# Two projection groups fed side by side, half rows of x first, and six warming products instead of eight

## The chip, the cores and the metric

One core of one Trainium2 chip. The metric is the device time of one execution in microseconds (us), the median of three runs. Engines: TensorE (PE in the profile) multiplies, ScalarE (ACT) and VectorE (DVE) work on tiles, GpSimd (POOL) does small work, SyncE (SP) issues most DMAs. PSUM has eight banks of 128 x 512 float32.

## The reference

A decoder block with two attention branches that read the same normalised input. What this case touches is its first step, the input projection:

```python
h = rms_norm(x, norm_g[layer])            # x: 512 x 1024
proj = h @ w_in[layer]                    # 1024 x 6152
fq, fk, fv, fz, mq, mk, mv, mz, ga, gb, fl = split_cols(proj, IN_SPLITS)
q = rms_norm(to_heads(fq, FOX_HEADS), fox_q_g[layer])
k = rms_norm(to_heads(fk, FOX_HEADS), fox_k_g[layer])
log_f = jax.nn.log_sigmoid((fl + b_f[layer]).astype(jnp.float32)).transpose(0, 2, 1)
...
merged = (jax.nn.sigmoid(ga + b_gate[layer, 0]) * (y_fox @ w_fox[layer])
          + jax.nn.sigmoid(gb + b_gate[layer, 1]) * (y_moba @ w_moba[layer]))
x = x + merged @ w_out[layer]
```

`fq` and `fk` are 512 columns each, `fl` is 8. All is float32.

## The kernel before

The hidden dimension of 1024 is cut into 8 slices of 128 rows (`KT`, index k), the sequence of 512 into 4 tiles of 128 (`NT`, index t), the columns of the weights into groups of 256 (`CW`). A group has a name: `fqa` is the first half of the columns of fq, `fka` the first half of fk, `fza`, `fzb` those of fz, `fva` of fv, and so on. `fka` carries the 8 columns of fl (tile `wfl`) too, so its products are 264 columns wide.

To keep float32 accuracy each operand is split into a high and a low part of type float32r, and each product is made of three: high x high, high x low, low x high. The high part of a weight chunk (`wh_...`) is a copy by ACT (or by DVE), the low part (`wl_...`) a subtraction by DVE; for x they are `Zh` (ACT, scaled by the norm weight) and `Zl` (DVE), one pair for each k (`split_x`, L121 to L126). The first three groups of columns use these un-normalised Z; the row statistics (`x_stats`, L218, from which `r` comes) are put in later: `norm_row` (L234, tile `p_rbc`) turns r into a row, and `normalise` (L240) makes `Gh` and `Gl`, which all later groups use.

`first_loads` (L65) issues the first DMAs: the constants `cs` on ACT's queue, all else on SP's, weight chunks of `fqa` (k=0, k=1, k=2 and 3, k=4 to 7) between the slices `xt` of x. Eight DMAs can be on their way: each later one waits until the one eight before it has landed. `first_split` (L148) makes the two parts of the fqa chunks, with `split_x` between them, `load_fl` (L139) loads and splits `fka` in two chunks of 4 slices. `first_qk` (L371) then runs over k, and for each k over the four t, with three products each, into four banks: first all of `fqa`, in the banks of the tags `pj` and `lg`, then all of `fka`, in the banks `tp` and `pv`. `evac_qk` (L307) copies each bank out on ACT; `fza` takes the `pj` banks next, `p_rbc` an `lg` bank, `fzb` a `tp` bank. Before the data are there, PE runs `WARM` = 8 products on a tile of zeros (L106).

The text of the program gives priorities; the order of instructions on each engine is then fixed by a scheduler when the program is built, and each engine takes its own in that order. Two places later in the program matter: `p_LR` (L489), which ends the forget gate's work and opens the attention of the first heads, and attention itself, where products of the next groups (`fqb`, `fkb`, ...) are put between as filling.

Of the kernel before, what the change touches and what calls it, by code (L numbers as in the profile page):

```python
# [7 lines left out]
F32 = mybir.dt.float32  # L8
F32R = mybir.dt.float32r
AF = mybir.ActivationFunctionType  # L10
OP = mybir.AluOpType
AX = mybir.AxisListType

P = 128
S = 512
D = 1024
NT = S // P
KT = D // P
HD = 64
CW = 256  # L20
EPS = 1e-6
NEG = -3.0e38
WARM = 8
WR = 4

C_NG, C_BG, C_FQ, C_FK, C_MQ, C_MK, C_BF, C_GQ, C_GK, C_END = 0, 8, 24, 25, 26, 27, 28, 36, 52, 68
# [3 lines left out]
def fox_moba_kernel(ctx: ExitStack, tc, xT, x, w_in, w_fl, w_fox, w_moba, w_out, cst, rope, out):  # L30


    nc = tc.nc
    V, A, G, T = nc.vector, nc.scalar, nc.gpsimd, nc.tensor

    con = ctx.enter_context(tc.tile_pool(name="con", bufs=1))
    sb = ctx.enter_context(tc.tile_pool(name="sb", bufs=1))
# [3 lines left out]
    stage = {}  # L41
# [7 lines left out]
    def t2(tag, bufs, name, shape=(P, 512), dt=F32):  # L49
        pool = stage["pool"] if tag in ("qs", "pt", "pc", "ys") else sb  # L50
        return pool.tile(list(shape), dt, name=name, tag=tag, bufs=bufs)

    def pst(tag, bufs, name):
        return ps.tile([P, 512], F32, name=name, tag=tag, bufs=bufs)
# [5 lines left out]
        return pst("tp", 3, name)  # L60


    XT, RAW = {}, {}

    def first_loads():  # L65
        def xt(eng, k):
            XT[k] = t2("y", 15, f"xt{k}")
            eng.dma_start(out=XT[k], in_=xT[:, k, :])

        def w(k0, k1):  # L70
            hf = k0 // 4
            if hf not in RAW:
                RAW[hf] = sb.tile([P, 4, CW], F32, name=f"wr_fqa{hf}", tag="wr", bufs=WR)
            nc.sync.dma_start(out=RAW[hf][:, k0 - 4 * hf:k1 - 4 * hf], in_=w_in[0, :, k0:k1, :])
        nc.scalar.dma_start(out=cs, in_=cst)
        w(0, 1)
        xt(nc.sync, 0)
        w(1, 2)
        xt(nc.sync, 1)
        w(2, 4)  # L80
        xt(nc.sync, 2)
        xt(nc.sync, 3)
        w(4, 8)
        for k in range(4, KT):
            xt(nc.sync, k)


    cs = con.tile([P, C_END], F32, name="cs")
# [16 lines left out]
    wps = pst("tp", 3, "warm_ps")  # L105
    for i in range(WARM):  # L106
        T.matmul(wps, warm[:, :P], warm, start=True, stop=True)
# [10 lines left out]
    Gl = con.tile([P, KT, S], F32R, name="Gl")  # L118
    Z = {}

    def split_x(*ks):  # L121
        for k in ks:
            xt = XT[k]
            zh, zl = Z[k] = [stage["pool"].tile([P, S], F32R, name=f"Z{hl}{k}") for hl in "hl"]
            A.activation(zh, xt, AF.Copy, scale=col(C_NG + k))
            V.scalar_tensor_tensor(zl, xt, col(C_NG + k), zh.bitcast(F32), op0=OP.mult, op1=OP.subtract)  # L126


    chunks = {}

    def split(src, n, name, half=False):
        hi = sb.tile([P, 4, 264], F32R, name=f"wh_{name}", tag="wh", bufs=4)
        lo = sb.tile([P, 4, 264], F32R, name=f"wl_{name}", tag="wl", bufs=4)
        A.activation(hi[:, :, 0:n], src, AF.Copy)  # L134
        for eng, q in ((V, slice(0, 2)), (G, slice(2, 4))) if half else ((V, slice(0, 4)),):
            eng.tensor_tensor(out=lo[:, q, 0:n], in0=src[:, q], in1=hi[:, q, 0:n].bitcast(F32), op=OP.subtract)  # L136
        return hi, lo

    def load_fl(name, c0, hf):  # L139
        raw = sb.tile([P, 4, CW], F32, name=f"wr_{name}{hf}", tag="qk", bufs=4)  # L140
        nc.sync.dma_start(out=raw, in_=w_in[c0 // CW, :, 4 * hf:4 * hf + 4, :])
        hi, lo = split(raw, CW, f"{name}{hf}")
        f = wfl[:, 4 * hf:4 * hf + 4, :]
        A.activation(hi[:, :, CW:264], f, AF.Copy)
        V.tensor_tensor(out=lo[:, :, CW:264], in0=f, in1=hi[:, :, CW:264].bitcast(F32), op=OP.subtract)
        chunks.setdefault(name, []).append((hi, lo))

    def first_split(hf, between):  # L148
        raw = RAW[hf]
        hi = sb.tile([P, 4, 264], F32R, name=f"wh_fqa{hf}", tag="wh", bufs=4)  # L150
        lo = sb.tile([P, 4, 264], F32R, name=f"wl_fqa{hf}", tag="wl", bufs=4)
        for q, xs in enumerate(between):
            k = slice(2 * q, 2 * q + 2) if hf else slice(max(q, 2 * q - 2), max(q + 1, 2 * q))
            if hf == 0 and q < 2:
                V.tensor_copy(hi[:, k, :CW], raw[:, k])
            else:
                A.activation(hi[:, k, :CW], raw[:, k], AF.Copy)
            V.tensor_tensor(out=lo[:, k, :CW], in0=raw[:, k], in1=hi[:, k, :CW].bitcast(F32), op=OP.subtract)
            split_x(*xs)
        chunks.setdefault("fqa", []).append((hi, lo))  # L160

    COLS = {}
    off = 0
    for nm in ("fq", "fk", "fv", "fz", "mq", "mk", "mv", "mz"):
        for hfn in ("a", "b"):
            COLS[nm + hfn] = off
            off += CW
    for nm in ("ga", "gb"):
        for i in range(4):
            COLS[f"{nm}{i}"] = off  # L170
            off += CW

# [17 lines left out]
    def stream(name):  # L192
        first_prep[name] = len(preps)
        if name[0] == "G":
            group(name)
            return
        w, n, cnt = ((w_fox, int(name[2]), 1) if name[:2] == "wf" else (w_moba, int(name[2]), 1) if name[:2] == "wm"
                     else (w_out, int(name[2]), 2) if name[:2] == "wo" else (w_in, COLS[name] // CW, 2))
        for hf in range(cnt):
# [18 lines left out]
    def x_stats():  # L218
        G.memset(mh, -0.5)
        for t in range(NT):  # L220
            for hf in range(2):
                xt = t2("y", 15, f"x{t}{hf}")
                nc.sync.dma_start(out=xt, in_=x[t * P:(t + 1) * P, hf * 512:(hf + 1) * 512])
                j = t2("u", 4, "junk")
                A.activation(j, xt, AF.Square, accum_out=ms2[:, t, hf:hf + 1])
        V.tensor_add(mm, ms2[:, :, 0], ms2[:, :, 1])
        V.tensor_scalar(mm, mm, 1.0 / D, EPS, op0=OP.mult, op1=OP.add)
        V.tensor_scalar(e2, mm, EPS, None, op0=OP.mult)
        G.tensor_tensor(out=r, in0=mm, in1=mh[:, :NT], op=OP.pow)
# [138 lines left out]
                        in1=tab[:, ts, None, 24:32].to_broadcast([P, 2, 4, 8]), op=OP.mult)  # L368
        G.tensor_tensor(out=qn[:, :, :, 0:16], in0=ra, in1=rb, op=OP.add)

    def first_qk(name, tags):  # L371
        banks = [pst(tg, n, f"{name}_{i}") for i, (tg, n) in enumerate(tags)]
        n = 264 if name == "fka" else CW
        for kk in range(KT):
            hi, lo = chunks[name][kk // 4]
            k = kk % 4
            for t in range(NT):
                st = slice(t * P, (t + 1) * P)
                T.matmul(banks[t][:, :n], Z[kk][0][:, st], hi[:, k, :n], start=(kk == 0), stop=False)
                T.matmul(banks[t][:, :n], Z[kk][0][:, st], lo[:, k, :n], start=False, stop=False)  # L380
                T.matmul(banks[t][:, :n], Z[kk][1][:, st], hi[:, k, :n], start=False, stop=(kk == KT - 1))
        return banks

    def unit(name, t):
        def go():
# [317 lines left out]
    def group(name):  # L703
# [201 lines left out]
    def seq(names):  # L905
        for u in filler(names):
            u()

    first_split(0, ((0,), (1, 2), (3, 4)))
    first_split(1, ((5, 6), (7,)))  # L910
    nc.sync.dma_start(out=wfl, in_=w_fl)
    load_fl("fka", COLS["fka"], 0)
    load_fl("fka", COLS["fka"], 1)
    b1 = first_qk("fqa", (("pj", 2), ("pj", 2), ("lg", 2), ("lg", 2)))
    b2 = first_qk("fka", (("tp", 3), ("tp", 3), ("tp", 3), ("pv", 1)))
    x_stats()
    for t in range(NT):
        evac_qk(b1[t], "fqa", t)
# [5 lines left out]
    fz = filler(["fza", "fzb"])  # L924
# [119 lines left out]
```

## Time and profile before

| | us |
|---|---|
| median of 3 runs (lowest, highest) | 433.29 (433.22, 433.48) |
| the profiled execution | 432.65 |
| its span | 430.9 |
| PE busy | 424.5 |
| DVE busy | 313.7 |
| ACT busy | 249.6 |
| POOL busy | 86.6 |
| DMA, mean rate over the span | 130 GB/s |

A span is the time from the first to the last record of the profiled execution. The page gives each engine's busy time, and a chain: the work that ended last, followed back from each step to what released it. A timeline row has start, length, engine, line, operation and the tiles written and read; in brackets stands how long the engine was idle before it, and what ended that. A matmul's listed length includes the time until its result is out, so consecutive products overlap in the list.

### The profile page before, as it was taken

The page shows a single profiled execution, that of the slowest core. Times are in us where ns is not written, and L with a number is a line of the kernel's source. Part 1 is how long each engine was busy: PE and PEld are TensorE (multiplying, and loading weights), DVE is VectorE, ACT ScalarE, POOL GpSimd, SP SyncE. Part 2 cuts the span into 40 slices and gives each one's busy share as a digit, 9 for nine tenths or more (in the row PEclk, how much of TensorE's full clock was granted, in tenths as well). Part 3 has the DMA queues.
Part 4 walks back from the last instruction along what each step waited for, and adds up shares of the span by engine and source line. Part 5 has one row for each costly group of instructions (what it writes and reads, how often), then busy time and mean ns, then how long its engine had stood idle before and what let it go on. Part 6 is the DMA issues. An engine that isn't in the chain of part 4 may idle for free.

```text
span 430.9 us, 8095 instructions
## 1 busy us (share of the span) xinstructions
PE 424.5 (99%) x3103; PEld 400.5 (93%) x3103; DVE 313.7 (73%) x559; ACT 249.6 (58%) x480; POOL 86.6 (20%) x108
## 2 busy tenths in 40 slices
PE   8999999999999999999999999999999999999996
PEld 6998899999999998999998878899999989999996
DVE  5679965869979867767856898959897796673311
ACT  4986336876868767677765855547655545531100
POOL 1049200227044660044630003020000000000000
PEclk9999999999999999999999999999999999999999
DMA  7981235326565413303304305561415306525221
GB/s 245 398 293 54 94 102 152 98 79 206 170 213 176 140 39 119 122 13 122 111 15 137 110 13 186 181 196 52 146 50 184 110 3 211 187 96 166 85 92 46
DMA packets 25670, 56.13 MB, mean 130 GB/s; under 512 B 3240, under 2 KB 11872, under 8 KB 25632
## 3 DMA queue, kind: packets, MB, share of 16 engines
q1 hardware_dynamic: 14528, 40.08, 28.0%
q10 hardware_dynamic: 9952, 11.34, 8.8%
q0 software_dynamic: 1152, 4.19, 2.7%
q8 instruction: 24, 0.39, 0.4%
q14 instruction: 14, 0.11, 0.1%
HBM read 46.01 MB, written 6.32 MB: 121 GB/s over the span
## 4 chain that ended last, share of the span: by engine, by line
PE 96%; DVE 2%; DMA 1%; issue 0%; SPq 0%; DVEq 0%
PE pb_GB L750 3%; PE pb_GA L750 3%; PE pb_GB L749 3%; PE pb_GA L747 3%; PE pb_GB L747 3%; PE pb_GA L749 3%; PE po L847 3%; PE po L849 3%; PE po L848 3%; PE pv L608 2%; PE pv L607 2%; PE lg L553 2%; PE lg L552 2%; PE pm L676 2%; PE pm L677 2%; PE pm L678 2%
## 5 line engine op out<-in xcount | busy, mean ns | idle before, releaser
L557 ACT ACTIVATE p<-p,negm 128x128 f32<-128x128 f32 (+1 forms) x64 | 35.7, 558 | 14.4 <-DVE negm L555 12.2
L331 POOL TENSOR_TENSOR ff<-ss,mh 128x8 f32<-128x8 f32 x16 | 27.8, 1743 | 65.5 <-DVE ss L329 65.1
L555 DVE CUSTOM_DVE_ANT_0 p<-lg,mask 128x128 f32<-128x128 f32 (+1 forms) x64 | 30.8, 485 | 13.0 <-PE lg L553 12.3
L847 PE MATMUL po<-wh_wo,mgh 128*128 128x256 f32 x96 | 27.1, 282 | 0.0
L849 PE MATMUL po<-wh_wo,mgl 128*128 128x256 f32 x96 | 27.0, 282 | 0.0
L848 PE MATMUL po<-wl_wo,mgh 128*128 128x256 f32 x96 | 26.9, 281 | 0.0
L857 DVE TENSOR_TENSOR ot<-po,xr 128x256 f32<-128x256 f32 x16 | 6.6, 424 | 24.7 <-PE po L849 23.5
L134 ACT ACTIVATE wh_wo<-wr_wo 128x1024 fp32r<-128x1024 f32 x8 | 8.5, 1061 | 21.6 <-PE po L849 8.0
L552 PE MATMUL lg<-KH,QS 128*128 128x128 f32 (+1 forms) x64 | 20.5, 329 | 0.0
L633 DVE TENSOR_TENSOR ypair<-pv,ysh 64x512 f32<-64x512 f32 x16 | 11.0, 687 | 12.9 <-ACT ysh L632 12.8
L136 DVE TENSOR_TENSOR wl_GB<-wr_gb,wh_GB 128x1024 fp32r<-128x1024 f32 x14 | 16.8, 1224 | 4.2 <-ACT wh_GB L134 3.3
L136 DVE TENSOR_TENSOR wl_GA<-wr_ga,wh_GA 128x1024 fp32r<-128x1024 f32 x14 | 17.9, 1294 | 2.5 <-ACT wh_GA L134 2.4
L134 ACT ACTIVATE wh_GB<-wr_gb 128x1024 fp32r<-128x1024 f32 x14 | 14.6, 1059 | 8.6 <-PE pm L677 2.5
L134 ACT ACTIVATE wh_GA<-wr_ga 128x1024 fp32r<-128x1024 f32 x14 | 14.6, 1059 | 8.5 <-PE pb_GA L749 4.3
L848 PEld LDWEIGHTS po<-wl_wo,mgh 128*128 128x128 f32 x96 | 18.1, 189 | 0.0
L849 PEld LDWEIGHTS po<-wh_wo,mgl 128*128 128x128 f32 x96 | 18.1, 189 | 0.0
L847 PEld LDWEIGHTS po<-wh_wo,mgh 128*128 128x128 f32 x96 | 18.1, 189 | 0.0
L136 DVE TENSOR_TENSOR wl_wo<-wr_wo,wh_wo 128x1024 fp32r<-128x1024 f32 x8 | 9.8, 1222 | 7.4 <-ACT wh_wo L134 7.4
L632 ACT ACTIVATE ysh<-pv 64x512 f32<-64x512 f32 x16 | 9.5, 594 | 8.9 <-PE pv L608 6.4
L604 DVE TENSOR_TENSOR ptl<-p_a,pth 128x512 fp32r<-128x512 f32 x16 | 11.0, 686 | 4.1 <-ACT pth L603 4.1
L676 PE MATMUL pf<-yhf,wh_wf 128*128 128x512 f32 x32 | 13.2, 414 | 0.6 <-DVE zs_mzb L422 0.6
L526 DVE SCALAR_TENSOR_TENSOR QS<-p_qT,cs,QS 64x512 fp32r<-64x512 f32 x16 | 12.0, 750 | 2.5 <-ACT QS L525 2.2
(447 smaller groups left out, 1769.9 us busy)
## 6 DMA issues: line engine op xcount, KB each, us to landing
wr_ga<-in_w_in_dram SPq DMA_DIRECT2D x8, 512.0 KB, 3.5
wr_gb<-in_w_in_dram SPq DMA_DIRECT2D x8, 512.0 KB, 5.0
wr_wo<-in_w_out_dram SPq DMA_DIRECT2D x8, 512.0 KB, 4.2
xt<-in_xT_dram SPq DMA_DIRECT2D x8, 256.0 KB
x<-in_x_dram SPq DMA_DIRECT2D x8, 256.0 KB, 7.2
KH<-KH ACTq DMA_DIRECT2D x16, 128.0 KB, 2.4
s_dramh<-sum_sh ACTq DMA_DIRECT2D x8, 256.0 KB
s_draml<-sum_sl ACTq DMA_DIRECT2D x8, 256.0 KB, 4.4
```

What stands on the lines that cost most here:

```text
L134: A.activation(hi[:, :, 0:n], src, AF.Copy)
L136: eng.tensor_tensor(out=lo[:, q, 0:n], in0=src[:, q], in1=hi[:, q, 0:n].bitcast(F32), op=OP.subtract)
L331: G.tensor_tensor(out=f2, in0=ss.rearrange("p t h -> p (t h)"), in1=mh, op=OP.pow)
L552: T.matmul(lg[:, :n], qs[:, qt], kh[:, :n], start=True, stop=False)
L555: V.tensor_tensor_reduce(pt, lg[:, :n], mask[:, 512 - n:512], -0.125, 3.0e38, op0=OP.add, op1=OP.min, accum_out=mkn[:, hh, i:i + 1])
L557: A.activation(pt, pt, AF.Exp, bias=mkn[:, hh, i:i + 1], scale=-1.0, accum_out=rs[:, hh, i:i + 1])
L747: T.matmul(o, hi[:, k, cc], lh, start=(n < 3 and c == 0 and k == 0), stop=False, skip_group_check=True)
L749: T.matmul(o, hi[:, k, cc], ll, start=False, stop=False, skip_group_check=True)
L750: T.matmul(o, lo[:, k, cc], lh, start=False, stop=(k == 3), skip_group_check=True)
L847: T.matmul(p[:, :CW], gh[:, st], hi[:, k, :CW], start=(kk == 0), stop=False)
L848: T.matmul(p[:, :CW], gh[:, st], lo[:, k, :CW], start=False, stop=False)
L849: T.matmul(p[:, :CW], gl[:, st], hi[:, k, :CW], start=False, stop=(kk == KT - 1))
```

## The change

`first_loads` issues the chunks of fqa and fka in turn, the first slice of x in two halves of 256 columns, and wfl on ACT's queue behind cs. `split_x` can work in parts, `first_split` takes one chunk of either group, `load_fl` is gone. `first_qk` does one k for both groups; the last loop goes through k, splits what that k needs and then issues its 24 products. All eight banks are taken at once. `WARM` is 6.

```diff
-WARM = 8
+WARM = 6
...
     def first_loads():
-        def xt(eng, k):
-            XT[k] = t2("y", 15, f"xt{k}")
-            eng.dma_start(out=XT[k], in_=xT[:, k, :])
-
-        def w(k0, k1):
+        def w(nm, k0, k1):
             hf = k0 // 4
-            if hf not in RAW:
-                RAW[hf] = sb.tile([P, 4, CW], F32, name=f"wr_fqa{hf}", tag="wr", bufs=WR)
-            nc.sync.dma_start(out=RAW[hf][:, k0 - 4 * hf:k1 - 4 * hf], in_=w_in[0, :, k0:k1, :])
+            if (nm, hf) not in RAW:
+                tag, bufs = ("wr", WR) if nm == "fqa" else ("qk", 4)
+                RAW[nm, hf] = sb.tile([P, 4, CW], F32, name=f"wr_{nm}{hf}", tag=tag, bufs=bufs)
+            nc.sync.dma_start(out=RAW[nm, hf][:, k0 - 4 * hf:k1 - 4 * hf],
+                              in_=w_in[0 if nm == "fqa" else COLS["fka"] // CW, :, k0:k1, :])
+
+        def xt(k, c0=0, c1=S):
+            if k not in XT:
+                XT[k] = t2("y", 15, f"xt{k}")
+            nc.sync.dma_start(out=XT[k][:, c0:c1], in_=xT[:, k, c0:c1])
         nc.scalar.dma_start(out=cs, in_=cst)
-        w(0, 1)
-        xt(nc.sync, 0)
-        w(1, 2)
-        xt(nc.sync, 1)
-        w(2, 4)
-        xt(nc.sync, 2)
-        xt(nc.sync, 3)
-        w(4, 8)
-        for k in range(4, KT):
-            xt(nc.sync, k)
+        nc.scalar.dma_start(out=wfl, in_=w_fl)
+        w("fqa", 0, 1)
+        xt(0, 0, 256)
+        xt(0, 256, S)
+        w("fka", 0, 1)
+        w("fqa", 1, 2)
+        xt(1)
+        w("fka", 1, 2)
+        w("fqa", 2, 4)
+        xt(2)
+        w("fka", 2, 4)
+        xt(3)
+        w("fqa", 4, 8)
+        xt(4)
+        w("fka", 4, 8)
+        for k in range(5, KT):
+            xt(k)
...
-    def split_x(*ks):
-        for k in ks:
-            xt = XT[k]
-            zh, zl = Z[k] = [stage["pool"].tile([P, S], F32R, name=f"Z{hl}{k}") for hl in "hl"]
-            A.activation(zh, xt, AF.Copy, scale=col(C_NG + k))
-            V.scalar_tensor_tensor(zl, xt, col(C_NG + k), zh.bitcast(F32), op0=OP.mult, op1=OP.subtract)
+    def split_x(k, parts=1):
+        xt = XT[k]
+        Z[k] = [stage["pool"].tile([P, S], F32R, name=f"Z{hl}{k}") for hl in "hl"]
+        n = S // parts
+        for c in (slice(i * n, (i + 1) * n) for i in range(parts)):
+            zh, zl = (z[:, c] for z in Z[k])
+            A.activation(zh, xt[:, c], AF.Copy, scale=col(C_NG + k))
+            V.scalar_tensor_tensor(zl, xt[:, c], col(C_NG + k), zh.bitcast(F32), op0=OP.mult, op1=OP.subtract)
...
+    def first_split(nm, k0, k1, on_v=False):
+        hf = k0 // 4
+        if len(chunks.setdefault(nm, [])) == hf:
+            hi = sb.tile([P, 4, 264], F32R, name=f"wh_{nm}{hf}", tag="wh", bufs=4)
+            lo = sb.tile([P, 4, 264], F32R, name=f"wl_{nm}{hf}", tag="wl", bufs=4)
+            chunks[nm].append((hi, lo))
+            if nm == "fka":
+                f = wfl[:, 4 * hf:4 * hf + 4, :]
+                A.activation(hi[:, :, CW:264], f, AF.Copy)
+                V.tensor_tensor(out=lo[:, :, CW:264], in0=f, in1=hi[:, :, CW:264].bitcast(F32), op=OP.subtract)
+        hi, lo = chunks[nm][hf]
+        k = slice(k0 - 4 * hf, k1 - 4 * hf)
+        raw = RAW[nm, hf]
+        if on_v:
+            V.tensor_copy(hi[:, k, :CW], raw[:, k])
+        else:
+            A.activation(hi[:, k, :CW], raw[:, k], AF.Copy)
+        V.tensor_tensor(out=lo[:, k, :CW], in0=raw[:, k], in1=hi[:, k, :CW].bitcast(F32), op=OP.subtract)
...
-    def first_qk(name, tags):
-        banks = [pst(tg, n, f"{name}_{i}") for i, (tg, n) in enumerate(tags)]
-        n = 264 if name == "fka" else CW
-        for kk in range(KT):
+    def first_qk(banks, kk):
+        for name, bank in banks.items():
+            n = 264 if name == "fka" else CW
             hi, lo = chunks[name][kk // 4]
             k = kk % 4
             for t in range(NT):
...
-    first_split(0, ((0,), (1, 2), (3, 4)))
-    first_split(1, ((5, 6), (7,)))
-    nc.sync.dma_start(out=wfl, in_=w_fl)
-    load_fl("fka", COLS["fka"], 0)
-    load_fl("fka", COLS["fka"], 1)
-    b1 = first_qk("fqa", (("pj", 2), ("pj", 2), ("lg", 2), ("lg", 2)))
-    b2 = first_qk("fka", (("tp", 3), ("tp", 3), ("tp", 3), ("pv", 1)))
+    banks = {nm: [pst(tg, n, f"{nm}_{i}") for i, (tg, n) in enumerate(tags)] for nm, tags in
+             (("fqa", (("pj", 2), ("pj", 2), ("lg", 2), ("lg", 2))), ("fka", (("tp", 3), ("tp", 3), ("tp", 3), ("pv", 1))))}
+    for k0, k1 in ((0, 1), (1, 2), (2, 4), (4, 8)):
+        first_split("fqa", k0, k1, k0 == 0)
+        for k in range(k0, k1):
+            split_x(k, 2 if k == 0 else 1)
+            if k == k0:
+                first_split("fka", k0, k1)
+            first_qk(banks, k)
+    b1, b2 = banks["fqa"], banks["fka"]
```

More of the change, by code (lines that the diff above doesn't have):

```diff
@@ L60, in tp @@
         return pst("tp", 3, name)
+    COLS = {}
+    off = 0
+    for nm in ("fq", "fk", "fv", "fz", "mq", "mk", "mv", "mz"):
+        for hfn in ("a", "b"):
+            COLS[nm + hfn] = off
+            off += CW
+    for nm in ("ga", "gb"):
+        for i in range(4):
+            COLS[f"{nm}{i}"] = off
+            off += CW
     XT, RAW = {}, {}
     def first_loads():
-        def xt(eng, k):
-            XT[k] = t2("y", 15, f"xt{k}")
-            eng.dma_start(out=XT[k], in_=xT[:, k, :])
-        def w(k0, k1):
+        def w(nm, k0, k1):
             hf = k0 // 4
-            if hf not in RAW:
-                RAW[hf] = sb.tile([P, 4, CW], F32, name=f"wr_fqa{hf}", tag="wr", bufs=WR)
-            nc.sync.dma_start(out=RAW[hf][:, k0 - 4 * hf:k1 - 4 * hf], in_=w_in[0, :, k0:k1, :])
-        nc.scalar.dma_start(out=cs, in_=cst)
-        w(0, 1)
-        xt(nc.sync, 0)
-        w(1, 2)
-        xt(nc.sync, 1)
-        w(2, 4)
-        xt(nc.sync, 2)
-        xt(nc.sync, 3)
-        w(4, 8)
-        for k in range(4, KT):
-            xt(nc.sync, k)
+            if (nm, hf) not in RAW:
[7 more added lines that the diff above has]
+            nc.sync.dma_start(out=XT[k][:, c0:c1], in_=xT[:, k, c0:c1])
+        nc.scalar.dma_start(out=cs, in_=cst)
+        nc.scalar.dma_start(out=wfl, in_=w_fl)
[15 more added lines that the diff above has]
+            xt(k)
     cs = con.tile([P, C_END], F32, name="cs")
@@ L137, in split @@
         return hi, lo
[L139 to L171, printed above, removed]
+    def first_split(nm, k0, k1, on_v=False):
[16 more added lines that the diff above has]
+        V.tensor_tensor(out=lo[:, k, :CW], in0=raw[:, k], in1=hi[:, k, :CW].bitcast(F32), op=OP.subtract)
@@ L378, in first_qk @@
                 st = slice(t * P, (t + 1) * P)
[L379 to L382, printed above, removed]
+                T.matmul(bank[t][:, :n], Z[kk][0][:, st], hi[:, k, :n], start=(kk == 0), stop=False)
+                T.matmul(bank[t][:, :n], Z[kk][0][:, st], lo[:, k, :n], start=False, stop=False)
+                T.matmul(bank[t][:, :n], Z[kk][1][:, st], hi[:, k, :n], start=False, stop=(kk == KT - 1))
     def unit(name, t):
```

## The prediction

> **What bounds the kernel now.** First the page: how much of the span each engine works, and the chain of work that ended last.
>
> ```profile
> span 430.9 us, 8095 instructions
> PE 424.5 (99%) x3103; PEld 400.5 (93%) x3103; DVE 313.7 (73%) x559; ACT 249.6 (58%) x480; POOL 86.6 (20%) x108
> PE 96%; DVE 2%; DMA 1%; issue 0%; SPq 0%; DVEq 0%
> ```
>
> TensorE (PE) is the bound: idle for 6.4 us in all. Only two things make this kernel faster: fewer products, or idle PE time taken away. The change touches no product but two warming ones, so the question is where PE idles near the start. The chain of waits in order of time begins so:
>
> ```profile
> 1.69 3.68 DMA wr_fqa<-in_w_in_dram
> 5.39 0.30 DVE wh_fqa L155
> 6.07 0.76 DVE Zl L126
> 6.86 0.74 PE fqa L381 x4
> ```
>
> The second weight chunk lands at 5.39, VectorE (DVE), in order, does that chunk's high and low part, and only then Zl0, for which PE waits. The timeline of the first 30 us (start, length, in brackets the idle time before and its releaser):
>
> ```profile
> 0.80 0.42 ACTq L75 DMA_DIRECT2D cs<-in_cst_dram  x1
> 3.52 0.30 DVE L155 CAST wh_fqa<-wr_fqa 128x256 fp32r<-128x256 f32 x1 [2.01 <-DMA wr_fqa<-in_w_in_dram]
> 3.85 0.42 DVE L158 TENSOR_TENSOR wl_fqa<-wr_fqa,wh_fqa 128x256 fp32r<-128x256 f32 x1
> 4.50 0.72 ACT L125 ACTIVATE Zh<-xt,cs 128x512 fp32r<-128x512 f32 x1 [1.75 <-DMA xt<-in_xT_dram]
> 5.27 0.19 PEld L379 LDWEIGHTS fqa<-wh_fqa,Zh 128*128 128x128 f32 x1 [0.66 <-ACT Zh L125]
> 6.80 0.72 ACT L125 ACTIVATE Zh<-xt,cs 128x512 fp32r<-128x512 f32 x1 [1.58 <-DMA xt<-in_xT_dram]
> 6.86 0.74 PE L381 MATMUL fqa<-wh_fqa,Zl 128*128 128x256 f32 x4 [0.39 <-DVE Zl L126]
> 7.58 0.39 PE L379 MATMUL fqa<-wh_fqa,Zh 128*128 128x256 f32 x1
> 15.56 0.28 PE L379 MATMUL fqa<-wh_fqa,Zh 128*128 128x256 f32 x1
> 17.68 0.28 PE L379 MATMUL fqa<-wh_fqa,Zh 128*128 128x256 f32 x1
> 18.04 0.53 PE L379 MATMUL fka<-wh_fka,Zh 128*128 128x264 f32 x3
> 19.14 0.28 PE L379 MATMUL fka<-wh_fka,Zh 128*128 128x264 f32 x1
> 29.37 0.28 PE L379 MATMUL fka<-wh_fka,Zh 128*128 128x264 f32 x1
> 29.73 0.39 PE L402 MATMUL pz_fza<-Zh,wh_fza 128*128 128x512 f32 x1
> ```
>
> Listed lengths of products overlap; the step from start to start is what PE takes. Between 15.56 and 17.68 lie 18 products of 256 columns: 0.118 us each. Between 19.14 and 29.37 lie 84 of 264 columns: 0.122 us each. The 96 products of fqa would take 96 x 0.118 = 11.3 us, but from 5.27 to 18.04 pass 12.8: **1.5 us of holes**, before which the first product waits for Zh0 until 5.27. From 18.04 on PE is dense. What can be won is the start and these holes.
>
> **The change part by part.** *Products side by side.* For every k the four fqa banks and then the four fka banks are fed, 24 products a k instead of 12: 12 x 0.118 + 12 x 0.122 = 2.88 us of work for each step of k. Data for one k is 262 kB of x and two weight chunks of 131 kB, 524 kB. The DMA supply (windows of 1 us; last columns granted clock, DMA share, GB/s):
>
> ```profile
> 1.00:2.00 1.00, 0.45 (x1) 0.45 (x2) 0.50 (x2) 0.75 (x1) 0.96 (x4) 1.00 0.08 24
> 2.00:3.00 1.00, 1.00 (x4) 0.72 (x4) 0.00 (x0) 0.74 (x2) 0.34 (x2) 1.00 0.84 210
> 3.00:4.00 1.00, 1.00 (x4) 0.81 (x3) 0.45 (x2) 0.00 (x0) 0.00 (x0) 1.00 0.97 241
> 4.00:5.00 1.00, 1.00 (x4) 0.52 (x2) 0.27 (x1) 0.50 (x1) 0.00 (x0) 1.00 0.80 181
> 5.00:6.00 1.00, 1.00 (x7) 0.73 (x7) 0.57 (x2) 0.22 (x1) 0.00 (x0) 1.00 0.94 248
> 6.00:7.00 1.00, 0.61 (x6) 0.41 (x5) 0.81 (x2) 0.20 (x1) 0.00 (x0) 1.00 0.98 328
> 7.00:8.00 1.00, 1.00 (x7) 0.82 (x8) 0.44 (x1) 0.88 (x2) 0.00 (x0) 1.00 0.96 354
> ```
>
> At 354 GB/s 524 kB take 1.5 us, half of PE's 2.88: once running, the products outlast their data. Only k=0 and k=1 can still wait.
>
> *When k=0 and k=1 land.* Summed, the rows give kB moved by a time: 24 at 2, 234 at 3, 475 at 4, 656 at 5, 904 at 6, 1232 at 7. Before, x0 was complete after cs 35 + 131 + 262 = 428 kB, which the curve passes at 3.80; ScalarE (ACT) took it up at 4.50, 0.7 later. For x1 (821 kB, 5.67, taken up at 6.80) the lag is 1.1. Now, with the head chunk wfl (33 kB) on ACT's queue beside cs: first fqa chunk 199 kB, x0's first half 330, second half 461, fka chunk 592, second fqa chunk 723, x1 985. So the first half is passed at 3.40 and taken up at about 4.2; its Zh is half of 0.72, or the 0.42 of DVE's 256-column row: 0.40. First product at 4.2 + 0.40 + 0.05 (5.27 - 4.50 - 0.72) = 4.65, against 5.27. wl for it is ready at 4.27 as before.
>
> x1 is passed at 6.25, taken up at 7.35 with the longer lag, Zh1 is done at 8.07: **k=1 starts at 8.1.** The 24 products of k=0 need 2.88 from 4.65, so about 0.6 us of waiting inside k=0 costs nothing: Zh0's second half, the fka chunk (passed at 4.65, taken up at 5.5, split at 5.9, when PE has ten products behind it at 5.85), and Zl0 in two halves. ACT's and DVE's extra instructions there hide behind x1; without that cover each costs its 0.4.
>
> *Rest of the stage.* From 8.1 follow 7 x 24 = 168 products: 84 x 0.118 + 84 x 0.122 = 20.2 us. fza starts at 28.3 instead of 29.73: **gain 1.4 to 1.5 us.** Bounds: if PE goes from k=0 into k=1 without a wait (start 4.5), it is 4.5 + 2.88 + 20.2 = 27.6, gain 2.1. If the five pieces of 1 KB rows ahead of x1 move at the worst row, 181 GB/s, from 2.0 on, x1 is passed at 7.3, taken up at 8.4, k=1 starts at 9.2, fza at 29.4, gain 0.3. The rows nearest to it (210, 241) are where I stand.
>
> *Six warming products.* One tile's row:
>
> ```profile
> L107 PE MATMUL warm_ps<-warm x8: 632/632/796, 1.5 to 4.7; 128*128 128x512 f32 x8
> ```
>
> Eight starts in 3.2 us are 0.457 apart; six free PE at about 4.3, before 4.65. Eight would free it at about 5.2, k=0 would end at 8.1, just when x1 is there: the edit is worth nothing by itself. Its price can be the clock. 512 columns at 0.118 per 256 should take 0.236; they took twice that, though the granted clock reads 1.00. At 5.27 the products run at full pace. The Trainium skill, in "TensorE: Matmul & The Clock Gate", Part 1, says that the array runs at half rate until it was busy for one free-running window of about 3.4 us; the trace agrees in the halved pace, and its 3.7 us from 1.55 to 5.27. Whether 2.7 us of warming and a short gap are enough, no row shows: a rival below.
>
> *What moves behind the stage.* fqa's evacuations ran under fka's products; now fqa bank 0 is complete 21 products (2.5 us) before the end, at about 25.7, and fza, which takes its bank, would otherwise wait.
>
> ```profile
> 18.04 0.63 ACT L310 ACTIVATE qn_fqa<-fqa 128x256 f32<-128x256 f32 x2
> 24.05 1.06 ACT L134 ACTIVATE wh_fza<-wr_fza 128x1024 fp32r<-128x1024 f32 x1 [0.21 <-DMA wr_fza<-in_w_in_dram]
> 34.63 0.60 PE L237 MATMUL p_rbc<-ident,r 128*128 128x128 f32 x4
> 36.20 0.68 DVE L417 TENSOR_TENSOR zs_fza<-pz_fza,rbc 128x512 f32<-128x512 f32 x1
> 50.97 1.28 DVE L244 TENSOR_TENSOR Gl<-xt,Gh 128x512 fp32r<-128x512 f32 x2
> 55.17 0.28 PE L305 MATMUL pj_fva<-wh_fva,Gl 128*128 128x256 f32 x1
> 66.19 0.60 PE L489 MATMUL p_LR<-ident,c 128*64 128x128 f32 x4
> ```
>
> ACT is through with wh_fza at 25.1, evacuates at 25.7 to 26.4 (0.32 each) and is ahead of 28.3: nothing, with 2 us of cover. p_rbc stands 32 products behind fza's start in the new order (21 before): 28.3 + 32 x 0.234 = 35.8, 1.1 us later than before; the last Gl comes at about 53.4 instead of 52.25. PE wants it 33 products into fva (fva1 is interleaved), near 54.9 (55.17 before), so 1.5 of 2.9 us are left: nothing. SP's queue keeps its order behind x7, POOL its own.
>
> **Sum.** The profiled execution took 432.65 us (span 430.9 and 1.75 around it); 432.65 - 1.45 = 431.2. It lies 0.64 under the median 433.29, so the median should become **431.8**.
>
> **The rivals.** *A, wfl blocks ACT.* ACT's queue has the wfl split between Zh0's halves, and all later splits stand behind it.
>
> ```profile
> wfl<-in_w_fl_dram SPq DMA_DIRECT2D x1, 32.0 KB, 5.7
> ```
>
> If it lands as slowly from ACT's queue (issue 1.2 + 5.7 = 6.9), Zh0's second half is there at 7.5, k=0 ends with 18 more products at 9.7, k=1 starts at 9.7, fza at 29.9: 433.5, no change. Against it: those 5.7 us were spent behind some 1.7 MB of x and weights in SP's queue, and cs, issued at 0.80 from ACT, was there by 4.50. The lesser form is slow 1 KB rows (gain 0.3, 433.0).
>
> *B, the clock stays halved.* If PE is not released by its first 2.7 us, products take 0.24 instead of 0.12 until a time T. To the next window, 3.4 us behind 5.27, T = 8.7: 17 products done by then, the other 7 of k=0 end at 9.5, k=1 starts 1.4 late: 433.2, no change. The page of the skill named above would allow it. For it: pace was never seen with less warming. Against: the gap from 4.3 to 4.65 is short, and the holes behind 5.27 did not bring the slow pace back.
>
> *C, slower: attention falls behind.* In the new order p_LR stands 33 products later, so attention starts at 66.19 - 1.45 + 33 x 0.118 = 68.6, 2.4 us later in time, while the filling products are used up earlier. Where DVE is full, it could not catch up:
>
> ```profile
> 100.00:110.00 10.00, 10.00 (x81) 9.82 (x81) 9.87 (x24) 5.51 (x13) 4.85 (x4) 1.00 0.67 207
> 110.00:120.00 10.00, 10.00 (x85) 9.91 (x84) 9.91 (x20) 8.67 (x17) 0.00 (x0) 1.00 0.65 201
> PE p_b L597 <- DVE ptl L604: 0.2, 1, 0.2
> ```
>
> If all the delay reaches PE, the end is 2.4 us later than before: 435.7. It decides once PE's waits in attention exceed 1.45. Against: PE waited there for DVE 0.2 us in all although DVE was 99% busy, as filling products covered it, and both orders agree again at the 1241st product (about 163 us). *D, not done as said*, the products not really interleaved: the built order has them k by k, fqa then fka; excluded.
>
> **How the numbers follow.** Forecast 0.70 (own range 431.1 to 432.4), A with slow rows 0.10, B 0.08, C 0.12 (0.09 of it slower, the rest no change). 0.2%, 0.87 us, is about what a measurement of this kernel tells from no change. Faster is the forecast and a little of A: 0.72; same 0.19; slower 0.09. The range goes from 431.0 (gain 2.3, just above the bound) to 433.3, to take in most of A and B; C's slow part and the worst of A stay out.
>
> **What would show it.** First fqa product near 4.65; a wait before k=1 until about 8.1, released by Zh1; no PE idle to 55; first pz_fza near 28.3. Start of pz_fza later than 29.4, with waits on wh_fka or Zh inside k=0, means A; product steps of 0.24 behind 4.65 mean B; PE waits on ptl, lg or KL between 70 and 130 mean C. A first product still at 5.2 makes the start wrong but not the sum, as long as x1 decides.

## The result and the profile after

| | before | after |
|---|---|---|
| median of six runs, side by side (us) | 433.25 | 437.83 |
| lowest, highest | 432.73, 433.48 | 436.6, 441.25 |
| the profiled execution, span | 432.65, 430.9 | 436.6, 434.9 |

The ratio is 1.0118, 95% interval 1.010 to 1.0136: slower by 4.6 us. The runs also lie 4.65 us apart where those of before lie 0.75 apart. From the page of after, the span, the engines' busy time and the shares of the chain (the work that ended last, followed back):

```profile
span 434.9 us, 8091 instructions
PE 424.8 (98%) x3101; PEld 400.1 (92%) x3101; DVE 313.4 (72%) x560; ACT 249.8 (57%) x483; POOL 92.5 (21%) x108
PE 62%; DVE 7%; issue 2%; DMA 1%; ACT 1%; ACTq 1%; DVEq 0%
```

PE works as long as before (424.8, 424.5) and is idle for 10.1 us instead of 6.4: the loss of the profiled execution is waiting. The chain's shares can't be set beside those of before: here they add to 74%, as the chain reaches back only to 109.9 us, while before's reaches back to the start. DVE has 7% of the span in this part alone, against 2% before. The first products in the timeline of after, and the start of fza:

```profile
4.74 0.58 PE L387 MATMUL fqa<-wh_fqa,Zh 128*128 128x256 f32 x1 [0.27 <-ACT Zh L148]
5.12 0.41 PE L388 MATMUL fqa<-wl_fqa,Zh 128*128 128x256 f32 x1
6.40 0.31 PE L388 MATMUL fqa<-wl_fqa,Zh 128*128 128x256 f32 x1
7.97 0.72 ACT L148 ACTIVATE Zh<-xt,cs 128x512 fp32r<-128x512 f32 x1 [1.22 <-DMA xt<-in_xT_dram]
8.75 0.39 PE L387 MATMUL fqa<-wh_fqa,Zh 128*128 128x256 f32 x1
28.95 0.39 PE L409 MATMUL pz_fza<-Zh,wh_fza 128*128 128x512 f32 x1
```

From 5.12 to 6.40 lie six products, 0.213 us each: half pace, hidden here because x1 is taken up only at 7.97. PE is dense from 8.75 on, and fza starts 0.78 us earlier than before (29.73). That gain is then lost. The statistics and DVE's queue, after:

```profile
24.36 1.06 ACT L157 ACTIVATE wh_fza<-wr_fza 128x1024 fp32r<-128x1024 f32 x1 [0.57 <-DMA wr_fza<-in_w_in_dram]
29.46 0.64 ACT L234 ACTIVATE junk<-x 128x512 f32<-128x512 f32 x1
37.93 0.68 DVE L424 TENSOR_TENSOR zs_fza<-pz_fza,rbc 128x512 f32<-128x512 f32 x1
56.94 1.21 DVE L159 TENSOR_TENSOR wl_fqb<-wr_fqb,wh_fqb 128x1024 fp32r<-128x1024 f32 x1
58.67 0.41 DVE L350 TENSOR_TENSOR v_fva<-pj_fva,v_fva 128x256 fp32r<-128x256 f32 x1
```

The same places in the timeline of before:

```profile
22.78 1.06 ACT L134 ACTIVATE wh_fza<-wr_fza 128x1024 fp32r<-128x1024 f32 x1 [0.51 <-DMA wr_fza<-in_w_in_dram]
27.46 0.63 ACT L225 ACTIVATE junk<-x 128x512 f32<-128x512 f32 x1 [1.03 <-DMA x<-in_x_dram]
57.84 0.42 DVE L341 TENSOR_TENSOR v_fva<-pj_fva,v_fva 128x256 fp32r<-128x256 f32 x1
```

The weights of fza are taken up 1.6 us later, the last square of x (`junk`) 2.0, the first `zs_fza` 1.7 (36.20 before). In the window from 24 to 30 us DVE works 5.3 us before and 3.4 after, where its low parts of fza and fzb wait for ACT's high parts. From `zs_fza` to 58 us DVE is never idle in either kernel, and so v_fva, the low part of the first v tile, comes 0.83 later. fva has two banks, so its third tile (called fva2 below) must wait for v_fva. fva starts 0.8 earlier (52.48 before, 51.67 after); 0.8 + 0.8 = 1.6, and PE's waits after say just that:

```profile
PE pj_fva L312 <- DVE v_fva L350: 1.6, 1, 1.6
PE pj_mqa L312 <- DVE v_fvb L350: 0.8, 1, 0.8
PE lg L559 <- DMA KH<-KH: 0.8, 1, 0.8
```

Columns: total, times, longest (us). The other two lie in the first attention group: mqa's products wait for a bank that VectorE reads, and `lg` (the attention scores) for a DMA of k. Windows from 110 to 165 us, before and then after (first columns length and PE's busy time, 55.00 and 53.17 us):

```profile
110.00:165.00 55.00, 55.00 (x439) 53.60 (x438) 46.43 (x101) 42.50 (x95) 22.83 (x30) 1.00 0.50 154
```

```profile
110.00:165.00 55.00, 53.17 (x424) 51.14 (x424) 46.25 (x99) 39.35 (x89) 28.72 (x31) 1.00 0.48 153
```

The first pz_mza starts at 165.9 instead of 162.1, 3.8 us late, and the spans end 4.0 us apart.

### The profile page after: what moved, and what is told of

Read it like the earlier page. It is cut to its first block, busy times and chain, and to the rows that moved or that the text cites. A ratio compares the mean times of both kernels' runs of the same rounds, so it can differ in the third digit from the quotient of the medians.

```text
span 434.9 us, 8091 instructions
## 1 busy us (share of the span) xinstructions
PE 424.8 (98%) x3101; PEld 400.1 (92%) x3101; DVE 313.4 (72%) x560; ACT 249.8 (57%) x483; POOL 92.5 (21%) x108
## 4 chain that ended last, share of the span: by engine, by line
PE 62%; DVE 7%; issue 2%; DMA 1%; ACT 1%; ACTq 1%; DVEq 0%
PE pb_GA L757 3%; PE pb_GB L754 3%; PE pb_GA L754 3%; PE pb_GA L756 3%; PE pb_GB L757 3%; PE pb_GB L756 3%; PE po L854 3%; PE po L856 3%; PE po L855 3%; PE pm L683 2%; PE pm L684 2%; PE pm L685 2%; PE pv L615 2%; PE pf L683 2%; PE pv L614 2%
## 5 line engine op out<-in xcount | busy, mean ns | idle before, releaser
L340 POOL TENSOR_TENSOR ff<-ss,mh 128x8 f32<-128x8 f32 x16 | 26.8, 1681 | 74.8 <-DVE ss L338 47.4
L159 DVE TENSOR_TENSOR wl_GA<-wr_ga,wh_GA 128x1024 fp32r<-128x1024 f32 x14 | 16.8, 1221 | 3.7 <-PE pb_GA L757 2.9
L559 PEld LDWEIGHTS lg<-KH,QS 128*128 128x128 f32 x64 | 12.1, 189 | 1.6 <-DMA KH<-KH 1.1
```

The lines of the kernel that those rows point to most:

```text
L340: G.tensor_tensor(out=f2, in0=ss.rearrange("p t h -> p (t h)"), in1=mh, op=OP.pow)
L559: T.matmul(lg[:, :n], qs[:, qt], kh[:, :n], start=True, stop=False)
```

## The experiments

Three theories, named as in the expectations. **T1**: the statistics and DVE's queue come late, PE waits at fva2. **T3**: in the new built order p_LR and attention's first `lg` stand later among PE's instructions (rows 438 and 490; 405 and 443 before), and this costs behind 65 us by itself. **T4**: the clock and the six warming products.

What all profiled executions show, in one table: the first pz_fza, PE's wait at fva2, the last start of a pj_fva product, the row of the first lg, the time from there to the first pz_mza, and the profiled time beside the median. In before the weight load of that product waited 0.2 us for v_fva, and PE itself less than 0.1.

| kernel | fza | wait | fva ends | lg at | fva to mza | profiled | median |
|---|---|---|---|---|---|---|---|
| before | 29.7 | 0 | 64.4 | 443 | 97.7 | 432.65 | 433.25 |
| after | 29.0 | 1.6 | 65.3 | 490 | 100.6 | 436.6 | 437.83 |
| e1 | 29.2 | 1.5 | 65.3 | 490 | 99.3 | 435.45 | 437.68 |
| e2 | 29.9 | 0 | 63.9 | 443 | 97.7 | 432.26 | 432.48 |
| e3 | 28.8 | 2.9 | 67.9 | 467 | 100.1 | 438.82 | 438.02 |
| e4 | 31.1 | 0.2 | 65.9 | 443 | 98.2 | 434.63 | 433.62 |
| e5 | 29.1 | 3.2 | 69.6 | 443 | 97.6 | 437.97 | 437.95 |
| e6 | 29.7 | 2.7 | 69.0 | 457 | 98.7 | 438.72 | 438.62 |
| e7 | 29.5 | 1.6 | 65.8 | 467 | 98.2 | 434.49 | 435.1 |
| e8 | 30.7 | 2.0 | 68.9 | 490 | 100.3 | 440.08 | 438.71 |
| e9 | 28.9 | 0.4 | 63.6 | 490 | 100.0 | 434.34 | 434.8 |
| e10 | 28.7 | 0.3 | 63.7 | 443 | 98.6 | 433.15 | 433.15 |
| e11 | 30.1 | 0 | 64.5 | 443 | 97.7 | 433.19 | 433.2 |
| e12 | 30.2 | 0 | 64.2 | 443 | 97.7 | 432.44 | 432.53 |
| e13 | 28.9 | 1.6 | 65.2 | 467 | 101.4 | 437.16 | 438.36 |
| e14 | 31.2 | 0.8 | 66.4 | 490 | 99.7 | 436.8 | 436.39 |
| e15 | 31.0 | 0 | 65.4 | 443 | 97.7 | 433.79 | 433.23 |
| e16 | 29.0 | 1.6 | 65.3 | 490 | 99.3 | 435.28 | 435.74 |
| e17 | 29.5 | 0 | 63.9 | 443 | 97.7 | 432.27 | 432.21 |
| e18 | 29.5 | 0 | 63.9 | 443 | 97.7 | 432.28 | 432.24 |

**The last row tile of x in its own buffer (e1 on after, e2 on before).**

```diff
-xt = t2("y", 15, f"x{t}{hf}")
+xt = (stage["pool"].tile([P, 512], F32, name="x_last") if 2 * t + hf == 7
+      else t2("y", 15, f"x{t}{hf}"))
```

> The kernel after, with one thing changed: the last row tile of x for the row statistics has a buffer of its own, so that its load waits for no other tile; in the built order p_rbc then stands at PE's 205th row instead of the 228th, while p_LR (438) and the first lg (490) keep their places. T1 (the statistics come late, VectorE is the bound from 36 to 58 us, all later loss follows from it): VectorE's zs_fza starts at about 35 us, the 1.6 us wait at fva2 goes, pz_mza starts at least 3 us earlier than 165.9, total 433 to 434.5. T3 (the later place of p_LR and lg in the order costs the 2 to 3 us between 110 and 165 by itself): only the 1.6 us go, pz_mza at about 164.3, total about 436.2. T4 (the clock): no change, 437.8.

> The kernel before with the same buffer: p_rbc at row 196 instead of 217, p_LR 391 instead of 405. T1: the DVE queue is no tighter than before and PE was not idle there, so it gains at most the 0.2 us wait at fva2 and the 6.4 us of idle PE stay: 433.0 to 433.3. T3: attention begins 14 products earlier, which is worth nothing either as PE is dense: the same. It shows whether the gain of e1 belongs to the change or to any kernel with that buffer.

e1: 437.68, as after. p_rbc came 5.1 us earlier (36.4 to 31.3), yet zs_fza started at 42.3 and v_fva at 58.8: DVE did other work first and was as full from 30 us on. So not the moment of the statistics but the sum of DVE's queue sets fva2; that half of T1 fell. e2: 0.9978 of before (0.9968 to 0.9987), better than expected, with v_fva at 56.8 and fva ending 0.5 earlier.

**The warming products (e3: after with `WARM = 8`; e4: before with `WARM = 6`).**

> The kernel after with eight warming products instead of six; in the built order p_LR moves from 438 to 425 and lg from 490 to 467. T4 (six warming products leave the clock low, in every run by some amount, and cause the loss and the spread): the first real products run at 0.118 us each, total 433 or less, with a spread under 1 us. T1: the first products start at about 5.2 and run at full pace, k=1 still starts at 8.7 with x1, the statistics come as late, the wait at fva2 stays: about 437.5. T3: p_LR 13 places and lg 23 places earlier, half of the loss behind 110 us comes back: about 436.5.

> The kernel before with six warming products instead of eight and hardly another order (p_LR 404 for 405, lg 443 for 443). T4: slower by 1 us or more, 434.5 to 437, with a wide spread between runs. T1 and T3: the first products take about 0.21 instead of 0.12 us each until about 6.4; PE has fewer than ten products before the wait for Zl0, so that most of it is hidden: 433.3 to 433.9.

e4 gives 1.0008 (0.9997 to 1.002), e3 438.02, near T1's 437.5: T4 is not the loss. But e3's waits show a second price. Windows of one microsecond around its wait of 2.9 us at fva2 (last columns granted clock, DMA share, GB/s):

```profile
59.00:60.00 1.00, 0.00 (x0) 0.00 (x0) 1.00 (x3) 0.03 (x1) 0.00 (x0) 1.00 0.92 315
60.00:61.00 1.00, 0.74 (x6) 0.74 (x7) 1.00 (x6) 0.00 (x0) 0.00 (x0) 1.00 0.67 205
61.00:62.00 1.00, 1.00 (x7) 1.00 (x7) 0.90 (x5) 0.00 (x0) 0.00 (x0) 0.62 0.97 254
63.00:64.00 1.00, 1.00 (x7) 1.00 (x6) 0.00 (x0) 0.00 (x0) 0.00 (x0) 0.50 0.19 78
65.00:66.00 1.00, 1.00 (x11) 1.00 (x10) 0.42 (x1) 0.31 (x1) 0.00 (x0) 1.00 0.00 0
```

After the wait the granted clock is 0.5 for some 3.4 us, and 7 products a microsecond pass instead of 11: fva ends 2.6 us later than after's, for a wait 1.3 longer. The waits of 2.0 (e8), 2.7 (e6) and 3.2 (e5) are followed by it too, those of 1.6 or less at this place are not. After waits 1.6, at the edge; four of its other runs (437.74 to 441.25) have a mean granted clock of 0.992 to 0.996, the profiled one 0.998. 3.4 us at half clock in 435 are 0.004 of the mean. That these runs lost the clock behind a wait is likely, but no trace of them was kept.

**Low parts of fqb on GpSimd (e5 on after, e6 on before).** In `split`, `G if name[:3] == "fqb" else V` for the subtraction.

> The kernel after with the low parts of the two fqb weight chunks (two subtractions of 1.21 us that stand in VectorE's full queue ahead of the first v_fva) made by GpSimd, which is idle there; in the built order p_LR comes to 404 and the first lg to 443, the places of the kernel before. T1 (VectorE's full queue between 30 and 58 us sets fva2, all later loss follows): v_fva at about 56.5 instead of 58.7, no wait at fva2, pz_mza at about 161.5, total 432.5 to 433.5. T4 (the clock and the first loads by themselves): 437 as after. T3 (order alone): the wait at fva2 goes as VectorE is relieved and the loss behind 110 us goes with the old places: it cannot be told from T1 by this run, only by the waits in its trace.

> The kernel before with the same two subtractions on GpSimd; p_LR at 382 for 405, lg at 457 for 443. T1: PE waited for VectorE in this stage only 0.2 us, so that the relief is worth little here: 432.5 to 433.2. If e5 comes out below this one, side by side projections are worth their 0.8 us once VectorE keeps up.

Both missed: 437.95 and 438.62. GpSimd's two subtractions in e6, and what VectorE did meanwhile:

```profile
50.84 4.21 POOL L136 TENSOR_TENSOR wl_fqb<-wr_fqb,wh_fqb 128x1024 fp32r<-128x1024 f32 x1 [7.75 <-ACT wh_fqb L134]
55.14 2.73 POOL L136 TENSOR_TENSOR wl_fqb<-wr_fqb,wh_fqb 128x1024 fp32r<-128x1024 f32 x1
```

```profile
51.51 1.28 DVE L244 TENSOR_TENSOR Gl<-xt,Gh 128x512 fp32r<-128x512 f32 x2
52.71 0.68 DVE L417 TENSOR_TENSOR zs_fzb<-pz_fzb,rbc 128x512 f32<-128x512 f32 x1
53.31 2.29 DVE L419 SCALAR_TENSOR_TENSOR zs_fza<-sg,zs_fza 128x512 f32<-128x512 f32 x1
55.52 2.39 DVE L463 SCALAR_TENSOR_TENSOR fg<-fg,fg 128x32 f32<-128x32 f32 x1
```

The two subtractions take GpSimd 4.2 and 2.7 us, where VectorE takes 1.2 for one. Beside them a VectorE operation of 0.68 us takes 2.29 and one of 0.18 takes 2.39; both have two operands in SBUF. The two subtractions `Gl` have two as well and took their usual time beside the first, longer one of GpSimd, so there it may be GpSimd that waited. The operation on `pz_fzb`, which reads PSUM, took its usual 0.68. The Trainium skill, in "SBUF — State Buffer", section "SBUF: two separate sides", states that a VectorE instruction with two SBUF inputs and a GpSimd one that reads SBUF exclude each other for the whole instruction, and that the one that starts later is blocked; the two slow rows agree with it. What these two are good for: e6 makes the kernel *before* 5.2 us slower (433.44 in that comparison) through a wait of 2.7 at fva2 and what follows it.

**1.8 us added to VectorE's queue, before (e7).**

```diff
     norm_row()
+    dly = stage["pool"].tile([P, S], F32, name="dly")
+    for _ in range(3):
+        V.tensor_tensor(out=dly, in0=rbc, in1=rbc, op=OP.subtract)
```

> The kernel before with three subtractions of 128x512 added on VectorE behind p_rbc (a result that nobody reads): 3 x 0.6 = 1.8 us more in its queue ahead of v_fva; in the built order p_LR comes to 426 and lg to 467. T1: v_fva at about 59.6, PE waits 1.8 to 2.0 us at fva2 with nothing else changed in loads, banks, warming products or interleaving, and the total is 435 to 438 with a wide spread, as after. T4: no effect on the clock's first microseconds, at most the 1.8 us: 433.5 to 435.

435.1, ratio 1.0036 (1.0023 to 1.005). Its v_fva (the row of its tile; the first and last start are 59.2 and 66.8):

```profile
L341 DVE TENSOR_TENSOR v_fva<-pj_fva,v_fva x4: 404/414/423, 59.2 to 66.8; 128x256 fp32r<-128x256 f32 x4
```

With nothing of the change in it, a wait of 1.6 us appears at fva2 and costs 1.7. It lacks after's further loss: 98.2 us from fva to mza. The spread was not wide (434.49 to 435.16).

**After's loads, products one group after the other (e8).**

```diff
-            first_qk(banks, k)
+            first_qk({"fqa": banks["fqa"]}, k)
+    for k in range(KT):
+        first_qk({"fka": banks["fka"]}, k)
```

> The kernel after with its loads and splits, but all 96 products of fqa first and then those of fka; p_rbc at 223, p_LR at 438, lg at 490. T1 with the loads as the cause of the late VectorE queue: zs_fza and v_fva as late as after (37.9 and 58.7), the wait at fva2 stays, and PE has its holes behind the first products again: 437 to 438.5. If the interleaving of the products (eight banks evacuated late) is the cause: v_fva back at 57.8, total 433.5 to 435.

438.71, v_fva at 60.8: the lateness is there without the interleaving, so it comes with what e8 keeps of the change: the loads, the splits and the eight banks taken at once.

**fqb's splits behind the second v_fva (e9 on after, e11 on before; e10 and e12 with the buffer of e1).** `pump` is called two steps less far ahead for the first two tiles of fva, and the splits of fqb get an order edge behind the last VectorE instruction issued:

```diff
-def go(i=first_prep[nm] + (n if nm[0] == "G" else 0), u=u):
+def go(i=first_prep[nm] + (n if nm[0] == "G" else -2 if nm == "fva" and n < 2 else 0), u=u):
...
+if name == "fqb":
+    with tc.issue_after(last_on(mybir.EngineType.DVE)):
+        chunks.setdefault(name, []).append(split(raw[0], CW, f"{name}{hf}"))
+    return
```

> The kernel after with both fqb weight chunks split only behind the second v_fva (nothing moved to another engine): 2.4 us less in VectorE's queue ahead of v_fva; p_LR (438) and the first lg (490) keep after's places. T1 (fva2's wait, with the halved clock that follows a wait of 2 us or more, and everything behind it, is the whole loss): v_fva at about 56.3, no wait at fva2, fva ends at about 63.6, pz_mza at about 161.5, total 432 to 433. T3 (the later places cost by themselves): fva ends at 63.6 too, but PE still waits at lg for KH and at pj_mqa, pz_mza comes at 163 to 164.5, total 434 to 435.5.

> e9 with the buffer for the last row tile of e1; in the built order p_LR comes to 400 and the first lg to 443, before's places. T1 and T3: neither loss, so that the 0.8 us won at the first products reach the end: pz_mza 161 to 161.5, total 432.0 to 432.8. If it stays above 434, both theories fall.

> The kernel before with e9's edit; p_LR 400, lg 443. There was no wait but 0.2 us to win: 432.7 to 433.4. The difference from e10 is what the side by side products are worth with the queue eased.

> The kernel before with e10's two edits; p_LR 400, lg 443. As e2 or a little better: 432.2 to 432.6. If e10 is below it, the change is worth having once VectorE's queue has room; if not, the change wins nothing at all.

e9: 434.8, 3.0 us below the six runs of after, by easing the one queue (0.9 below the two later runs of after, see e16). v_fva starts at 57.5, later than the 56.3 expected; fva ends at 63.6 as expected. Its order is still after's, and PE now waits longer at lg:

```profile
PE lg L563 <- DMA KH<-KH: 1.7, 1, 1.7
PE pj_fva L316 <- DVE v_fva L354: 0.4, 1, 0.4
```

e10, with lg at 443: 433.15, ratio 1.0001 (0.999 to 1.0012), so another 1.65 and no loss left, but not the 432.0 to 432.8 expected. What it won at the start did not reach the end: against e12 it is 1.5 us ahead at fza, 0.5 where fva ends, and 0.4 behind at mza, with 0.6 of waiting at lg. e12 (0.9986, 0.9976 to 0.9996) is below it, e11 equals before.

**p_LR earlier, the wait kept (e13).** The splits of fkb get such an edge behind the last forget row (`c4`).

```diff
+        FGL.append(last_on(mybir.EngineType.DVE))
         pl = tp("p_LR")
...
+if name == "fkb":
+    with tc.issue_after(FGL[0]):
```

> The kernel after with the two splits of the fkb weights ordered behind the last forget row on VectorE: p_LR comes to 415 and the first lg to 467 (438 and 490 in after; before 405 and 443); the queue ahead of v_fva is untouched. T1 (the wait at fva2, with a halved clock where it reaches 2 us, is the whole loss): the wait of 1.6 to 2 us stays, total 437 to 438. T1 with T3 (the later places cost about 2 us beside it): the wait stays, fva ends at 65.3 or with a halved clock at 67, but pz_mza comes 1 to 1.5 us nearer, total 435.5 to 437.

438.36, no gain, near T1's 437 to 438. Two of its waits:

```profile
PE pj_mqa L316 <- DVE v_fvb L354: 1.8, 1, 1.8
PE pj_fva L316 <- DVE v_fva L354: 1.6, 1, 1.6
```

The wait at lg is gone, one of 1.8 at mqa has come, with the clock at 0.5 from 117 to 119 us behind it. So T3 holds only for the order as a whole: in the table all kernels with lg at 443 take 97.6 to 98.6 us from fva to mza, those at 490 take 99.3 to 100.6, those at 467 anything from 98.2 to 101.4. Which of the instructions in those orders costs is not settled.

**Larger first pieces (e14), with e10's two edits (e15), and eight or ten warming products (e17, e18).**

```diff
         w("fqa", 0, 1)
-        xt(0, 0, 256)
-        xt(0, 256, S)
-        w("fka", 0, 1)
-        w("fqa", 1, 2)
+        xt(0)
+        w("fka", 0, 2)
         xt(1)
-        w("fka", 1, 2)
-        w("fqa", 2, 4)
+        w("fqa", 1, 4)
...
-            split_x(k, 2 if k == 0 else 1)
+            split_x(k)
```

> The kernel after with x0 in one piece and the first weights in larger pieces (fqa 0, fka 0 and 1 together, fqa 1 to 3 together, then as before): two pieces of 1 KB rows instead of six, same bytes. If the small rows slow the supply: over 340 GB/s from 6 to 14 us instead of 200 to 310, wh_fza on ScalarE at about 23 instead of 24.4, v_fva at about 57, wait at fva2 0 to 0.5, total 434.5 to 436 (the order, 438 and 490, still costs). If the supply is slowed by something else (the eight banks, the number of tiles): v_fva at 58.7 again, 437 to 438.

> e14 with e10's two edits (fqb splits behind the second v_fva, a buffer for the last row tile); p_LR 400, lg 443. If supply, queue and order are the whole story: side by side products win their 0.8 to 1.2 us here, 431.6 to 432.4, below the kernel before and below e12. If not below 432.9, side by side products win nothing even with all three eased.

> e15 with eight warming products instead of six. In e15's profile PE idled 1.17 us between the sixth warming product and the first real one, and the first 24 products then ran at 0.21 us instead of 0.12 until 10.8 us: about 2 us, and e15's runs lie in two groups, 431.2 to 431.6 and 433.0 to 433.8. If the gap behind the shorter warming does that: full pace from about 6 us on, the upper group goes, median 431.2 to 431.8, below every kernel so far. If the two groups come from something else: as e15, 433.2.

> e15 with ten warming products: they reach to about 5.8 us, past the arrival of the first data at 5.6. Full pace from the first product on, which starts 0.2 us later; x1 still decides k=1: 431.2 to 431.8 as e17, or 0.2 us above it. If even here the time is 433, the clock is not what splits e15's runs.

The supply, before, after and e18, from 5.6 to 14 us:

```profile
5.60:14.00 8.40, 8.02 (x62) 7.38 (x61) 6.92 (x12) 6.30 (x11) 0.00 (x0) 1.00 1.01 373
```

```profile
5.60:14.00 8.40, 8.28 (x66) 8.07 (x66) 4.11 (x9) 4.13 (x7) 0.00 (x0) 1.00 0.94 303
```

```profile
5.60:14.00 8.40, 8.09 (x63) 7.68 (x64) 5.42 (x10) 5.45 (x12) 0.00 (x0) 1.00 1.00 324
```

The larger pieces regain part of the rate (e14: 328, and 400 GB/s from 14 to 24 us, where before has 398 and after 372); the rest is not explained. v_fva is at 56.2 in e18, 57.1 in e10, whose order has the same places. e14 itself took 436.39, with v_fva at 60.1, between its two expectations: its start is late, as a wait of 1.4 us stands ahead of Zh0. e15 took 433.23, which its expectation reads as nothing won; its timeline shows what such a gap does:

```profile
1.54 2.93 PE L125 MATMUL warm_ps<-warm 128*128 128x512 f32 x6 [1.54 <-DVE fg_pre L477]
5.64 0.58 PE L389 MATMUL fqa<-wh_fqa,Zh 128*128 128x256 f32 x1 [1.17 <-ACT Zh L145]
7.30 0.41 PE L390 MATMUL fqa<-wl_fqa,Zh 128*128 128x256 f32 x1
10.79 0.31 PE L391 MATMUL fka<-wh_fka,Zl 128*128 128x264 f32 x1
```

All of k=0 runs at 0.21 us a product, until 10.8. Ten warming products, e18:

```profile
5.72 0.38 PE L389 MATMUL fqa<-wh_fqa,Zh 128*128 128x256 f32 x1 [0.17 <-ACT Zh L145]
5.94 0.28 PE L390 MATMUL fqa<-wl_fqa,Zh 128*128 128x256 f32 x1
6.54 0.28 PE L389 MATMUL fqa<-wh_fqa,Zh 128*128 128x256 f32 x1
```

Steps of 0.12 from 5.94 on, and e15's two groups (431.21 to 431.63, 433.0 to 433.79) become one, 432.09 to 432.44. e17's profile still has half pace to 7.8, hidden before k=1. Both are 1.0 us below before (0.9978 and 0.9976, intervals 0.9967 to 0.9989), above the 431.2 to 431.8 expected. e2, which is before with the buffer alone, has 0.9978 too: by the medians, no kernel with products side by side is shown to be faster than that. e15's lower group, four of its twelve runs, is faster still; what made it is not known.

**After once more (e16).**

> The kernel after once more, unchanged, for a second profile. The first profile was the fastest of seven runs (436.6) with a wait of 1.6 us at fva2 and full clock. T1: in a run of 437.5 or more the wait is 2 us or longer and the clock is halved for about 3.3 us behind it.

435.28 and 436.19, 2.6 us above before (1.0057, 1.0037 to 1.0077) instead of 4.6, neither above 437: what the expectation says of such runs stays open. The wait at fva2 is 1.6 again and fva ends at 65.3 again, but the stretch to mza is 1.3 shorter, without the wait at mqa: attention's waits vary from run to run.

## Why the prediction was wrong

It said 431.8 in a range of 431.0 to 433.3, faster at 0.72; 437.83 was measured. By its steps:

- *First product at 4.65*: 4.74, right. *Full pace behind six warming products*: wrong for about eight products, as rival B had it, at no cost here, since x1 was later.
- *x1 taken up at 7.35, k=1 at 8.1, fza at 28.3*: 7.97, 8.75 and 28.95. The mechanism was right, the term mis-sized was the supply: windows of 0 to 5 and 5 to 10 us have 151 and 260 GB/s, those of before 131 and 336, and the sum used before's rates with the smaller pieces. A gain of 0.78 instead of 1.45, inside the bounds of 0.3 to 2.1; it lies toward rival A's lesser form. Rival A itself did not come: ACT took up wfl's part at 4.60.
- *"p_rbc stands 32 products behind fza's start ... 35.8"*: 36.4, right but for fza's later start, 28.95 + 32 x 0.234 = 36.4. It did not wait for `r`, which GpSimd had ready at 31.9. The last Gl, forecast for 53.4, was done at 54.0, and PE did not wait for it.
- *The step that failed: "1.5 of 2.9 us are left: nothing."* It followed VectorE's lateness to the last Gl and stopped there. Some ten instructions further in the same full queue stands v_fva, for which fva2 waits; there the slack was already nothing, and in after PE waits there for 1.6 us. The trace of before has the row, under the tile v_fva, who waited for it (a weight load, PEld):

```profile
  PEld pj_fva L303: 0.2, 1
```

  What PE comes earlier and VectorE later is paid there: 0.8 and 0.8 us in after. e7 shows that 1.8 us more work in this queue makes before lose 1.7, and e9 that with 2.4 us taken out of it after's wait falls from 1.6 to 0.4 and fva ends 1.7 us earlier.
- *Rival C*, attention behind, was right in kind: p_LR came at 70.9 (68.6 forecast), and 1.65 us separate e9 from e10. Its chance of 0.12 rested on PE's waiting only 0.2 us in attention before, "as filling products covered it"; its other half, that the filling products are used up earlier, may have weighed more; no run separates the two. Its price of 2.4 was of the right size; the waits came at lg and mqa, not at ptl.

## What to carry to other kernels

When a stage is made faster, follow the engine that is full in the next stage, instruction by instruction, until a consumer on the bound engine has slack; a weight load's wait of 0.2 us in the old profile marked a place without any. A busy share of 98% on the bound engine does not mean that others have time to spare: VectorE worked over 99% of the time from 36 to 58 us. And where a scheduler orders the program, compare the built orders far behind the edit: the 1.65 us between e9 and e10 came back only with the order (the buffer by itself, e1, had given nothing). Last, try what eases the new kernel on the old one too: before gained 0.9 us from the buffer alone (e2).

## What the runs showed of the hardware

- A wait of 2.0 us on TensorE (e8) was followed by about 3.4 us at a granted clock of 0.5, and so was one of 1.8 (e13); waits of 1.5 to 1.7 in the middle of the kernel (e9's at lg among them) were not. The Trainium skill, "TensorE: Matmul & The Clock Gate", section "Why this matters for your kernels", advises no idle gaps over about 3 us; here shorter ones were enough.
- With six warming products and a gap of 1.2 us the halved pace lasted 5.2 us (e15), though the granted clock's column reads 1.00 there; with ten and 0.17 us it did not appear.
- Two VectorE instructions with both operands in SBUF stood still beside a GpSimd subtraction that reads SBUF: 0.18 became 2.39 us, 0.68 became 2.29 (e6).
